# Hybrid decoder step on one Trainium2 core: the order of the first tiles, GpSimd for the sample row, two bursts of decode products, and the last norm

## The chip, the cores and the metric

The kernel runs on one core of one Trainium2 chip. The metric is device time in microseconds of one execution. TensorE (PE) multiplies, VectorE (DVE) and ScalarE (ACT) work on tiles in SBUF and PSUM, GpSimd (POOL) has a queue of stores and some small operations, SyncE (SP) has the queue of most loads. Each engine takes its instructions in a fixed order and waits on semaphores.

## The reference

One layer of a hybrid decoder, for a prompt of 1024 tokens and for 8 samples of one new token each, both with the same weights:

```python
hn = rmsnorm(x, g_norm)                        # x: 1024 x 1024 (prompt), 8 x 1024 (samples)
u = hn @ w_in                                  # 1024 -> 7176 columns
xa, za, uq, uk, uv, uo, zb, ui, uf = split(u)  # seven groups of 1024, two of 4 (gates)
yA = rglru_branch(xa, ...)                     # gated linear recurrence, conv of width 4
h = mlstm_seq(q, k, v, ig, lf, C, n, m)        # 4 heads, chunks of 128 tokens
yB = rmsnorm_per_head(sigmoid(uo) * h) * g_mhead
merged = concat[yA * silu(za), yB * silu(zb)]
x = x + merged @ w_out                         # 2048 -> 1024
y = rmsnorm(x, g_final)
```

Outputs are y and the new states, all in float32.

## The kernel before

**Precision and products.** A float32 product is made of three products of parts (`mm3`, lines 64 to 68: high by high, high by low, low by high). Each operand is split first (`split`, lines 70 to 74): ScalarE casts the high part, VectorE subtracts it to get the low part. The large projections use a Strassen-like scheme of seven block products (`Q_P1` to `Q_P7`) instead of eight, for which sums of the operands' blocks are formed, and split as well.

**Who sets the order.** The program is traced in the order of the Python code, and a planner then gives each engine its fixed order from the tracing order (earlier is more urgent), from data and buffer dependencies and from its own guess of durations. An instruction that is ready in the planner's reckoning may be taken ahead of an earlier one that isn't. `tc.issue_after(ins)` puts what is traced in its block behind `ins` on the engine of `ins`; `tc.manual_schedule` keeps the instructions of its block in tracing order on the engines named, though others may come between them. A pool's tag with n buffers makes the next tile of that tag wait until an older one has been read for the last time.

**The opening (lines 403 to 603).** The prompt is eight tiles of 128 rows, the samples a ninth (number 8, eight rows), taken in the order `xorder = [4, 0, 8, 5, 1, 6, 2, 7, 3]`. For each: `x_fetch` loads it (SP; every third one in a single buffer "xb", the others in the six buffers "ws"); `x_stats` squares and sums on ScalarE and makes the inverse root on both engines; `x_turn` scales by root and norm row on VectorE, then transposes it on PE, in two halves of four blocks, into PSUM; `x_split` splits both halves; `x_copy` keeps plain copies of tiles 4 to 7; `plain` multiplies with the first unit's weights (two value heads, 264 and 256 columns, the first with the 8 gate columns) as 48 products; `x_combos` forms the Strassen sums and splits them. PSUM for the transposes rotates over "kv", "kv", "s", "qp". The norm row is broadcast over the partitions by a product into PSUM (`pb`), and copied to `gn_b` by ScalarE (line 577).

After the ninth tile, the samples' gate product (`pgd`, lines 594 to 599) and `dec_unit(0)` (the samples' products with the first unit's raw weights: 32 matmuls, 64 records in the trace) follow, and then the loads of the next unit's raw weights, whose buffers `dec_unit(0)` reads. In the trace, PE takes the pieces of `dec_unit` where they fit.

**The units (lines 1707 to 1770).** Thirteen more column groups of w_in, seven block products each, with splitting (`prep`), recurrence and decode work between them.

**Attention and output (from line 1774).** The heads and chunks n = 4 to 31 with output products as filling (`fill`). `wo_dec` (lines 1519 to 1529) multiplies the samples' rows with four raw row blocks of w_out at a time, in four column groups of PE at once, and adds the result to a buffer in DRAM. It is called at n = 19 and n = 21. `last_tile` (lines 1646 to 1671) ends the program: last output tile in three column parts (`LP`), sum of squares in three parts, inverse root by logarithm, exponential and one Newton step (`rsqrt_log`), scaling, store.

Of the kernel before, what the change touches and what calls it, by code (L numbers as in the profile page):

```python
# [17 lines left out]
P = 128  # L18
T = 1024
# [32 lines left out]
def hymba_kernel(  # L52
# [17 lines left out]
    def split(hi, lo, src):  # L70

        a = A.copy(hi, src)  # L72
        V.tensor_tensor(lo, src, hi.bitcast(F32), op=ALU.subtract)  # L73
        return a

# [125 lines left out]
    def rsqrt_mean(out, v, t, n):  # L201

        V.tensor_scalar(v, v, 0.25 / n, 0.25 * EPS, op0=ALU.mult, op1=ALU.add)
        rsqrt(out, v, t)

    def rsqrt_log(out, v, t):

        A.activation(t, v, AF.Ln, scale=2.0 ** 32)
        A.activation(out, t, AF.Exp, scale=-0.5)
# [230 lines left out]
    def x_stats(i):  # L440
        n = rows_of(i)
        junk = fp.tile([P, T], BF16, tag="junk", name="junk")
        A.activation(junk[:n], xt[i][:n], AF.Square, accum_out=st0[:n, i, 0:1])
        rsqrt_mean(st0[:n, i, 1:2], st0[:n, i, 0:1], st0[:n, i, 2:3], T)

    def x_turn(m):
        i = xorder[m]
        n = rows_of(i)
        xps[i] = []
        for half in range(2):  # L450
            hs = slice(half * HT, (half + 1) * HT)
            if m == 0 or half == 0:
                s = hs if m == 0 else slice(0, T)
                g = pb[half] if m == 0 else gn_b[:n, s]
                scaled = V.scalar_tensor_tensor(xt[i][:n, s], xt[i][:n, s], st0[:n, i, 1:2], g, op0=ALU.mult, op1=ALU.mult)
            pt = ps(("kv", "kv", "s", "qp")[(2 * m + half) % 4], [P, 4, P])
# [27 lines left out]
    def x_combos(i):  # L484

        p0, p1 = xps[i]
        s = slice(i % 4 * P, (i % 4 + 1) * P)
        f0, f1 = bf["f"]

        def out(q, t):  # L490
            split(cb[q][0][:, :, s], cb[q][1][:, :, s], t)
        if i >= 4:
            t3 = sg([P, 4, P], "t3")
            V.tensor_tensor(t3, f1, f0, op=ALU.subtract)
            out(Q_P7, t3)
        else:
            t1, t2, t4 = (sg([P, 4, P], f"t{n}") for n in (1, 2, 4))
            V.tensor_tensor(t1, f0, p0, op=ALU.subtract)
            V.tensor_tensor(t2, f1, t1, op=ALU.subtract)
            V.tensor_tensor(t4, p1, t2, op=ALU.subtract)  # L500
            out(Q_P6, t2)
            out(Q_P5, t1)
            out(Q_P4, t4)
# [6 lines left out]
    def w1_split(b):  # L510

        t = ws([P, 4, 256], f"w1h{b}"), ws([P, 4, 256], f"w1l{b}")
        split(t[0], t[1], raws[0, b][:, :, 256:512])
        w1.append(t)

# [23 lines left out]

    pw = ps("tr", [P, P])  # L540
# [22 lines left out]
    for m, i in enumerate(xorder):  # L563
        scaled = x_turn(m)
        if m == 0:
            def w0_split(k):
                split(hi[:, k:k + 2, 0:256], lo[:, k:k + 2, 0:256], raws[0, k // 4][:, k % 4:k % 4 + 2, 0:256])
            with tc.issue_after(root.ins), tc.issue_after(scaled.ins):
                w0_split(0)
                split(hi[:, :, 256:264], lo[:, :, 256:264], wg)  # L570
                x_split(i, 0)
                w0_split(2)
            with tc.issue_after(x_split(i, 1).ins):
                w0_split(4)
                w0_split(6)
                for half in range(2):
                    A.copy(gn_b[:, half * HT:(half + 1) * HT], pb[half])
                x_stats(xorder[1])
                for b in range(2):
                    w1_split(b)  # L580
        else:
            x_split(i, 0)
            x_split(i, 1)
        if 4 <= i < 8:
# [5 lines left out]
        if i < 8:  # L590
            plain(i)
            x_combos(i)

    pgd = ps("o", [32, 8])
    for k in range(KC):
        TE.matmul(pgd, hnd[:, NB * k:NB * k + 32], wg[:, k, :], start=k == 0, stop=k == KC - 1)
    gd = dconst([NB, 8], "gd")
    V.tensor_tensor(gd, pgd[0:NB], bgate[0:NB], op=ALU.add)
    ld(d_gd, gd)
    dec_unit(0)  # L600
    load_raw(1, 0)
    load_raw(1, 1)
# [916 lines left out]
    def wo_dec(ms):  # L1519

        po = ps("tr", [P, 512])
        with tc.manual_schedule(engines={mybir.EngineType.PE}):
            for m in ms:
                md = mAd[:, NB * (m % 8):NB * (m % 8) + 32]
                for half in range(2):
                    g = 2 * (m % 2) + half
                    TE.matmul(po[32 * g:32 * g + 32, :], md, oraw[m][:, half * 512:(half + 1) * 512], start=m < ms[2],  # L1527
                              stop=m >= ms[2], skip_group_check=True)
# [117 lines left out]
    def last_tile():  # L1646
# [19 lines left out]
        V.tensor_scalar(ms[:, 0:1], ms[:, 0:1], ms[:, 2:3], 0.25 / T, op0=ALU.add, op1=ALU.mult)  # L1666
        rsqrt_log(ms[:, 4:5], ms[:, 0:1], ms[:, 5:6])
# [112 lines left out]
    for n in range(4, N):  # L1780
# [21 lines left out]
        elif h == 1:  # L1802
            m_zg(c - 1)
            if n == N2 + 3:
                wo_dec((12, 13, 14, 15))
# [12 lines left out]
        else:  # L1818
            fill(1)
            if n == N2 + 1:  # L1820
                wo_dec((8, 9, 10, 11))
# [52 lines left out]
```

## Time and profile before

| | |
|---|---|
| median of three timed runs | 911.5 us (911.31 to 911.98) |
| the profiled execution's own time | 909.62 us |
| its span, first to last instruction | 907.8 us |
| TensorE busy | 895.5 us (99%), clock granted 0.998 |
| VectorE, ScalarE, GpSimd busy | 740.4 (82%), 586.1 (65%), 194.9 us (21%) |

The page's span is shorter than the execution's time by what lies before the first and behind the last instruction. A busy TensorE need not be at its peak: its instructions overlap, so that the distance from one start to the next tells more than a duration. A row of the timeline has start, duration, engine, line, operation, output and inputs, shapes and count, and in brackets the engine's idle time before it and who ended it. A row of a table by stretches has the stretch, its length, then the busy time and the count of instructions of each engine asked for, the granted TensorE clock (1.00 is full), the share of the DMA engines and GB/s.

### The profile page before, as it was taken

To read this page: it belongs to the slowest core of one execution; us is meant where nothing else is said; L and a number is where in the kernel's file an instruction comes from. 1 tells how busy PE (TensorE), PEld (TensorE's weight loads), DVE (VectorE), ACT (ScalarE), POOL (GpSimd) and SP (SyncE) were. 2 spreads that over 40 slices of the span, in tenths; PEclk is the share of its full clock that TensorE was granted. 3 is DMA by queue.
4 is the path that set the end of the run, shared out by engine and by line. 5 is a ranking of instruction groups with operands and counts; after the bars stand their busy time and mean duration, and the time that the engine had idled before them with its cause. 6 is when DMAs were issued, how large, how long until landed. Compare 5 with 4: busy or idle time off the path is not lost. (4 is left out here: it accounts for less than half of the span.)

```text
span 907.8 us, 16671 instructions
## 1 busy us (share of the span) xinstructions
PE 895.5 (99%) x5889; PEld 764.4 (84%) x5889; DVE 740.4 (82%) x1528; ACT 586.1 (65%) x1086; POOL 194.9 (21%) x322
## 2 busy tenths in 40 slices
PE   8999999999999999999999999999999999999996
PEld 6997778887888998888889998887788888888885
DVE  6974779869689978798999877679998779888973
ACT  7663446767667776576768775547787568556652
POOL 1111113012222222323333244010111111111120
PEclk9999999999999999999999999999999999999999
DMA  6412457347556557657585555536689889856531
GB/s 200 152 62 92 140 155 262 112 154 233 192 188 217 179 176 235 202 158 243 188 272 191 193 179 189 170 124 226 202 228 256 203 224 287 216 144 178 178 123 70
DMA packets 127037, 167.76 MB, mean 185 GB/s; under 512 B 17212, under 2 KB 94084, under 8 KB 126946
## 3 DMA queue, kind: packets, MB, share of 16 engines
q1 hardware_dynamic: 105334, 103.68, 37.1%
q0 software_dynamic: 21616, 63.02, 21.6%
q8 instruction: 46, 0.75, 0.4%
q14 instruction: 37, 0.30, 0.1%
q10 hardware_dynamic: 4, 0.00, 0.0%
HBM read 108.00 MB, written 62.92 MB: 188 GB/s over the span
## 5 line engine op out<-in xcount | busy, mean ns | idle before, releaser
L72 ACT CAST wh<-raw 128x1024 fp32r<-128x1024 f32 x91 | 95.4, 1049 | 72.8 <-DVE raw L299 21.2
L73 DVE TENSOR_TENSOR wl<-raw,wh 128x1024 fp32r<-128x1024 f32 x91 | 111.1, 1221 | 36.7 <-ACT wh L72 21.4
L66 PE MATMUL ps_X<-cb_hi,wh 128*128 128x512 f32 x320 | 126.6, 396 | 0.0
L68 PE MATMUL ps_X<-cb_hi,wl 128*128 128x512 f32 x320 | 125.4, 392 | 0.0
L67 PE MATMUL ps_X<-cb_lo,wh 128*128 128x512 f32 x320 | 125.1, 391 | 0.0
L66 PEld LDWEIGHTS ps_X<-cb_hi,wh 128*128 128x128 f32 x320 | 60.1, 188 | 15.9 <-issue 2.5
L68 PEld LDWEIGHTS ps_X<-cb_hi,wl 128*128 128x128 f32 x320 | 60.1, 188 | 13.3 <-issue 0.6
L67 PEld LDWEIGHTS ps_X<-cb_lo,wh 128*128 128x128 f32 x320 | 60.1, 188 | 12.8 <-issue 0.8
L66 PE MATMUL ps_Y<-cb_hi,wh 128*128 128x512 f32 x160 | 63.6, 398 | 0.3 <-DVE s L350 0.3
L68 PE MATMUL ps_Y<-cb_hi,wl 128*128 128x512 f32 x160 | 62.5, 391 | 0.0
L67 PE MATMUL ps_Y<-cb_lo,wh 128*128 128x512 f32 x160 | 62.5, 391 | 0.0
L66 PE MATMUL ps_X<-wh,cb_hi 128*128 128x256 f32 x192 | 54.8, 286 | 0.0
L67 PE MATMUL ps_X<-wl,cb_hi 128*128 128x256 f32 x192 | 54.4, 283 | 0.0
L68 PE MATMUL ps_X<-wh,cb_lo 128*128 128x256 f32 x192 | 54.4, 283 | 0.0
L66 PE MATMUL ps_o<-wo,mh 128*128 128x512 f32 (+1 forms) x136 | 53.1, 391 | 0.0
L68 PE MATMUL ps_o<-wo,ml 128*128 128x512 f32 (+1 forms) x136 | 51.6, 380 | 0.0
L67 PE MATMUL ps_o<-wo,mh 128*128 128x512 f32 (+1 forms) x136 | 51.5, 379 | 0.0
L66 PEld LDWEIGHTS ps_X<-wh,cb_hi 128*128 128x128 f32 x192 | 36.8, 191 | 1.5 <-ACT Z L279 0.4
L67 PEld LDWEIGHTS ps_X<-wl,cb_hi 128*128 128x128 f32 x192 | 36.8, 192 | 0.2
L68 PEld LDWEIGHTS ps_X<-wh,cb_lo 128*128 128x128 f32 x192 | 36.8, 192 | 0.0
L66 PEld LDWEIGHTS ps_Y<-cb_hi,wh 128*128 128x128 f32 x160 | 30.2, 188 | 6.9 <-DVE s L350 0.7
L68 PEld LDWEIGHTS ps_Y<-cb_hi,wl 128*128 128x128 f32 x160 | 30.0, 188 | 6.5
(573 smaller groups left out, 2746.9 us busy)
## 6 DMA issues: line engine op xcount, KB each, us to landing
raw<-in_w_in_dram SPq DMA_DIRECT2D x55, 512.0 KB
Cb<-in_state_mlstm_C_dram SPq DMA_DIRECT2D x32, 256.0 KB
out_dram<-Cb POOLq DMA_DIRECT2D x32, 256.0 KB, 5.0
qk<-d_qk SPq DMA_DIRECT2D x32, 256.0 KB
ring<-d_ro SPq DMA_DIRECT2D x26, 256.0 KB
d_qk<-s POOLq DMA_DIRECT2D x24, 256.0 KB, 4.4
d_x<-s POOLq DMA_DIRECT2D x16, 256.0 KB, 2.5
zsr<-d_y SPq DMA_DIRECT2D x16, 256.0 KB
```

The costliest lines, as they stand in the source:

```text
L66: TE.matmul(out, ah, bh, start=first, stop=False, skip_group_check=True)
L67: TE.matmul(out, ah, bl, start=False, stop=False, skip_group_check=True)
L68: TE.matmul(out, al, bh, start=False, stop=last, skip_group_check=True)
L72: a = A.copy(hi, src)
L73: V.tensor_tensor(lo, src, hi.bitcast(F32), op=ALU.subtract)
```

## The change

- The norm row's two copies go from ScalarE to VectorE, behind the low half of the last weight split. Tile 0's statistics and the splits of the second weight (`w1_split`) get explicit places: the second split stands behind tile 0's root, tile 4's copies and its value copies behind the second split.
- The loop over the tiles is written out for tiles 4, 0 and 5, with statistics of tile 5 behind tile 0's splits, and of tile 1 there too. The samples move behind tile 1: they are multiplied by norm row and root on GpSimd (`x_scale8`), transposed into a buffer of their own ("tr"), and copied by ScalarE. Since they share "xb" with tile 6, that tile's load now depends on them. PSUM for the prompt's tiles alternates between two pairs.
- `x_combos` is parted in `x_sums` and `x_outs`: the sums of tiles 0 and 4 are formed after tile 5's splits, and all splits of sums come one tile later.
- `samples()`, right after tile 1's products, holds `dec_unit(0)` and the gate product in one manually ordered block, the gate store and the loads of unit 1's raw weights.
- `wo_dec` is called once, at n = 21, for all eight row blocks.
- In `last_tile`, the logarithm takes the last part sum directly, with a scale and a bias made from the first two parts; the sum itself is formed beside it, for the Newton step.

```diff
-    def x_turn(m):
+    def x_scale(i, s, g):
+        return V.scalar_tensor_tensor(xt[i][:, s], xt[i][:, s], st0[:, i, 1:2], g, op0=ALU.mult, op1=ALU.mult)
+
+    def x_scale8():
+
+        G.tensor_tensor(xt[8][:NB], xt[8][:NB], gn_b[:NB], op=ALU.mult)
+        G.tensor_scalar(xt[8][:NB], xt[8][:NB], st0[:NB, 8, 1:2], None, op0=ALU.mult)
+
+    def x_turn(m, scale=True):
...
-            pt = ps(("kv", "kv", "s", "qp")[(2 * m + half) % 4], [P, 4, P])
+            if i == 8:
+                if half == 0:
+                    both = ps("tr", [P, 2, 4, 64])
+                pt = both[:, half]
+            else:
+                pt = ps(("kv", "kv", "s", "qp")[(2 * (m - (m > 2)) + half) % 4], [P, 4, P])
...
-            V.tensor_copy(blocks(hnd)[:, 4 * half:4 * half + 4], p[:, :, 0:NB])
+            A.copy(blocks(hnd)[:, 4 * half:4 * half + 4], p[:, :, 0:NB])
...
+    def samples():
+
+        pgd = ps("o", [32, 8])
+        with tc.manual_schedule(engines={mybir.EngineType.PE}):
+            dec_unit(0)
+            for k in range(KC):
+                TE.matmul(pgd, hnd[:, NB * k:NB * k + 32], wg[:, k, :], start=k == 0, stop=k == KC - 1)
+        gd = dconst([NB, 8], "gd")
+        V.tensor_tensor(gd, pgd[0:NB], bgate[0:NB], op=ALU.add)
+        ld(d_gd, gd)
+        load_raw(1, 0)
+        load_raw(1, 1)
...
+    with tc.issue_after(x_split(4, 1).ins):
+        w0_split(4)
+        w0_split(6)
+        with tc.issue_after(low[0].ins):
+            for half in range(2):
+                V.tensor_copy(gn_b[:, half * HT:(half + 1) * HT], pb[half])
+        root = x_stats(0)
+        w1_split(0)
+        with tc.issue_after(root.ins):
+            w1_last = w1_split(1)
+    x_fetch(3)
+    with tc.issue_after(w1_last.ins):
+        x_copy(4)
+        plain(4)
+    x_turn(1)
+    x_split(0, 0)
+    second = x_split(0, 1)
+    x_fetch(4)
+    with tc.issue_after(second.ins), tc.issue_after(low[0].ins):
+        x_stats(5)
+    plain(0)
+    with tc.issue_after(second.ins), tc.issue_after(low[0].ins):
+        x_stats(1)
+    x_turn(3)
+    for m in range(3, 9):
+        i = xorder[m]
+        if m > 3:
+            x_turn(m, m > 4)
+        x_split(i, 0)
+        second = x_split(i, 1)
+        if m == 3:
+            with tc.issue_after(second.ins), tc.issue_after(low[0].ins):
+                x_scale(1, slice(0, T), gn_b)
+                x_stats(8)
+                x_scale8()
+                due = [x_sums(0), x_sums(4)]
+                x_fetch(5)
+        if i >= 4:
             x_copy(i)
         if m + 3 < 9:
             x_fetch(m + 3)
         if m + 2 < 9:
             x_stats(xorder[m + 2])
+        if m == 4:
+            x_turn(2, False)
+            for half in range(2):
+                x_split(8, half)
+        if m > 3:
+            for d in due:
+                x_outs(*d)
+            due = [x_sums(i)]
+        plain(i)
+        if m == 3:
+            due.append(x_sums(i))
+        if m == 4:
+            samples()
+    for d in due:
+        x_outs(*d)
...
-        V.tensor_scalar(ms[:, 0:1], ms[:, 0:1], ms[:, 2:3], 0.25 / T, op0=ALU.add, op1=ALU.mult)
-        rsqrt_log(ms[:, 4:5], ms[:, 0:1], ms[:, 5:6])
+                V.tensor_scalar(ms[:, 0:1], ms[:, 0:1], 0.25 / T, None, op0=ALU.mult)
+                V.tensor_scalar(ms[:, 3:4], ms[:, 0:1], 2.0 ** 32, None, op0=ALU.mult)
+        A.activation(ms[:, 5:6], ms[:, 2:3], AF.Ln, scale=0.25 / T * 2.0 ** 32, bias=ms[:, 3:4])
+        V.tensor_scalar(ms[:, 0:1], ms[:, 2:3], 0.25 / T, ms[:, 0:1], op0=ALU.mult, op1=ALU.add)
+        newton(ms[:, 4:5], ms[:, 0:1], ms[:, 5:6])
...
             if n == N2 + 3:
-                wo_dec((12, 13, 14, 15))
+                wo_dec(range(8, 16))
...
-            if n == N2 + 1:
-                wo_dec((8, 9, 10, 11))
```

`newton` is `rsqrt_log` without its first line, the logarithm.

More of the change, by code (lines that the diff above doesn't have):

```diff
@@ L72, in split @@
         a = A.copy(hi, src)
-        V.tensor_tensor(lo, src, hi.bitcast(F32), op=ALU.subtract)
+        low[:] = [V.tensor_tensor(lo, src, hi.bitcast(F32), op=ALU.subtract)]
         return a
+    low = []
     cpool = ctx.enter_context(tc.tile_pool(name="cpool", bufs=1))
@@ L203, in rsqrt_mean, with newton @@
         V.tensor_scalar(v, v, 0.25 / n, 0.25 * EPS, op0=ALU.mult, op1=ALU.add)
-        rsqrt(out, v, t)
+        return rsqrt(out, v, t)
     def rsqrt_log(out, v, t):
         A.activation(t, v, AF.Ln, scale=2.0 ** 32)
+        newton(out, v, t)
+    def newton(out, v, t):
         A.activation(out, t, AF.Exp, scale=-0.5)
@@ L443, in x_stats @@
         A.activation(junk[:n], xt[i][:n], AF.Square, accum_out=st0[:n, i, 0:1])
[L444 to L446 removed]
+        return rsqrt_mean(st0[:n, i, 1:2], st0[:n, i, 0:1], st0[:n, i, 2:3], T)
+    def x_scale(i, s, g):
[4 more added lines that the diff above has]
+    def x_turn(m, scale=True):
         i = xorder[m]
@@ L449, in x_turn @@
         xps[i] = []
+        scaled = None
         for half in range(2):
             hs = slice(half * HT, (half + 1) * HT)
[L452 to L455, printed above, removed]
-            pt = ps(("kv", "kv", "s", "qp")[(2 * m + half) % 4], [P, 4, P])
+            if m == 0:
+                scaled = x_scale(i, hs, pb[half])
+            elif half == 0 and scale:
+                scaled = x_scale(i, slice(0, T), gn_b)
+            if i == 8:
[4 more added lines that the diff above has]
+                pt = ps(("kv", "kv", "s", "qp")[(2 * (m - (m > 2)) + half) % 4], [P, 4, P])
             for q in range(4):
@@ L482, in x_copy, with x_sums @@
             A.copy(f, p)
-    def x_combos(i):
+    def x_sums(i):
         p0, p1 = xps[i]
-        s = slice(i % 4 * P, (i % 4 + 1) * P)
         f0, f1 = bf["f"]
-        def out(q, t):
-            split(cb[q][0][:, :, s], cb[q][1][:, :, s], t)
         if i >= 4:
@@ L494, in x_combos, with x_outs @@
             V.tensor_tensor(t3, f1, f0, op=ALU.subtract)
[L495 to L503, printed above, removed]
+            return i, [(Q_P7, t3)]
+        t1, t2, t4 = (sg([P, 4, P], f"t{n}") for n in (1, 2, 4))
+        V.tensor_tensor(t1, f0, p0, op=ALU.subtract)
+        V.tensor_tensor(t2, f1, t1, op=ALU.subtract)
+        V.tensor_tensor(t4, p1, t2, op=ALU.subtract)
+        return i, [(Q_P6, t2), (Q_P5, t1), (Q_P4, t4)]
+    def x_outs(i, sums):
+        s = slice(i % 4 * P, (i % 4 + 1) * P)
+        for q, t in sums:
+            split(cb[q][0][:, :, s], cb[q][1][:, :, s], t)
     hi = fp.tile([P, KC, 264], F32R, tag="wph", name="wph")
@@ L512, in w1_split @@
         t = ws([P, 4, 256], f"w1h{b}"), ws([P, 4, 256], f"w1l{b}")
-        split(t[0], t[1], raws[0, b][:, :, 256:512])
         w1.append(t)
+        return split(t[0], t[1], raws[0, b][:, :, 256:512])
     gs = dconst([P, NCH, 8], "gs")
@@ L562, in hymba_kernel, with w0_split @@
     root = x_first_stats()
[L563 to L584, printed above, removed]
+    def w0_split(k):
+        split(hi[:, k:k + 2, 0:256], lo[:, k:k + 2, 0:256], raws[0, k // 4][:, k % 4:k % 4 + 2, 0:256])
@@ new lines, in hymba_kernel @@
+    scaled = x_turn(0)
+    with tc.issue_after(root.ins), tc.issue_after(scaled.ins):
+        w0_split(0)
+        split(hi[:, :, 256:264], lo[:, :, 256:264], wg)
+        x_split(4, 0)
+        w0_split(2)
+    with tc.issue_after(x_split(4, 1).ins):
[8 more added lines that the diff above has]
+            w1_last = w1_split(1)
@@ L589, in hymba_kernel @@
             x_stats(xorder[m + 2])
[L590 to L602, printed above, removed]
+        if m == 4:
[13 more added lines that the diff above has]
+        x_outs(*d)
     es_f.close()
@@ L1526, in wo_dec @@
                     g = 2 * (m % 2) + half
-                    TE.matmul(po[32 * g:32 * g + 32, :], md, oraw[m][:, half * 512:(half + 1) * 512], start=m < ms[2],
-                              stop=m >= ms[2], skip_group_check=True)
+                    TE.matmul(po[32 * g:32 * g + 32, :], md, oraw[m][:, half * 512:(half + 1) * 512], start=m < 10,
+                              stop=m >= 14, skip_group_check=True)
         dec_put(po, accum_op=ALU.add)
```

## The prediction

> **What bounds the kernel now.** I read the page first: its span, its engines.
>
> ```profile
> span 907.8 us, 16671 instructions
> ...
> PE 895.5 (99%) x5889; PEld 764.4 (84%) x5889; DVE 740.4 (82%) x1528; ACT 586.1 (65%) x1086; POOL 194.9 (21%) x322
> ```
>
> TensorE is busy for 99% of the span; what moves the end is PE time. It can be saved in two ways: PE stands idle less, or it does the same work with fewer costly switches. So next come the stretches around the change, PE alone.
>
> ```profile
> 14.16:20.47 6.31, 4.63 (x35) 1.00 0.12 45
> 20.47:72.42 51.95, 51.87 (x472) 1.00 0.33 106
> 72.42:81.40 8.98, 8.90 (x94) 1.00 0.46 137
> ```
>
> The second column is length, then PE's busy time. Idle shows in the first stretch alone, 6.31 - 4.63 = 1.68 us. The timeline tells why.
>
> ```profile
> 10.87 1.08 ACT L577 COPY gn_b<-ps_o 128x512 f32<-128x512 f32 x2
> ...
> 11.82 1.08 ACT L443 ACTIVATE junk<-x 128x1024 bf16<-128x1024 f32 x1
> ...
> 12.87 1.05 ACT L72 CAST w1h<-raw 128x1024 fp32r<-128x1024 f32 x1
> ...
> 13.02 0.15 DVE L203 TENSOR_SCALAR st<-st 128x1 f32<-128x1 f32 x1 [1.15 <-ACT junk L443]
> ...
> 13.96 1.23 DVE L73 TENSOR_TENSOR w1l<-raw,w1h 128x1024 fp32r<-128x1024 f32 x1 [0.78 <-ACT w1h L72]
> 14.04 0.28 PE L68 MATMUL ps_o<-wph,cb_lo 128*128 128x264 f32 x1
> ...
> 14.16 0.28 PE L66 MATMUL ps_o<-w1h,b12h 128*128 128x256 f32 x1
> ...
> 15.24 0.39 PE L67 MATMUL ps_o<-w1l,b12h 128*128 128x256 f32 x1 [0.79 <-DVE w1l L73]
> ...
> 17.51 1.26 DVE L455 SCALAR_TENSOR_TENSOR x<-x,st,gn_b 128x1024 f32<-128x1024 f32 x1
> ...
> 18.79 1.06 ACT L443 ACTIVATE junk<-x 128x1024 bf16<-128x1024 f32 x1
> 18.83 0.66 PE L459 MATMUL ps_s<-idF,x 128*128 128x128 f32 x4 [0.35 <-DVE x L455]
> ...
> 20.47 0.39 PE L66 MATMUL ps_o<-wph,cb_hi 128*128 128x264 f32 x1 [0.54 <-ACT cb_hi L72]
> ```
>
> PE starts a product every 0.12 us (14.04 to 14.16), then stands three times: for the low half of the second weight (15.24), for the scaled tile 0 (18.83), for its cast (20.47). Each traces back to ScalarE doing the norm row's copies at 10.87 first, and squaring tile 5 at 18.79 before tile 0's cast.
>
> **The change, part by part.**
>
> *Norm row on VectorE, sums apart (14 to 25 us).* The copies (1.08 us) leave ScalarE; VectorE has 1.15 us idle at the same place (the 13.02 row), and two copies of 512 from PSUM should fit there as they did on ScalarE: cost nothing, the cover being that hole. Tile 0's square moves from 11.82 to 10.87, w1h from 12.87 to 11.8 at best. But its data must be there:
>
> ```profile
> DMA  1999996101675116971911461111010021013970
> ```
>
> In this row (first 80 us in 40 slices) the DMA engines are full until 12 us. So w1h gains between nothing and 1.07; I take 0.8, a cast from about 12.05. Then w1l ends near 14.4 instead of 15.2, the second w1l near 16.1, and the scaling of tile 0, no longer behind tile 4's difference of 0.6 us, ends near 17.45 instead of 18.77. Transposes start near 17.6 instead of 18.83; the square of tile 5 now stands behind tile 0's second cast, so the cast starts 0.65 after the first transpose and not 1.0. First product of tile 0: near 18.9 instead of 20.47, -1.6 us. Bounds: -0.3 (weights late) and -1.68 (all the idle).
>
> *Tile 5 and the first unit's decode products (25 to 72 us).*
>
> ```profile
> 26.89 1.28 DVE L455 SCALAR_TENSOR_TENSOR x<-x,st,gn_b 128x1024 f32<-128x1024 f32 x1
> 27.22 1.06 PE L274 MATMUL ps_tr<-raw,hnd 128*32 128x128 f32 x26
> ...
> 28.32 0.63 PE L459 MATMUL ps_s<-idF,x 128*128 128x128 f32 x4
> ```
>
> Tile 5 is scaled only at 28.17, since VectorE splits tile 0's sums first; PE fills the hole with decode pieces. With the sums put off, tile 5 is scaled by about 23. The pieces, by stretch, line 274 alone, the last row a later unit's whole burst:
>
> ```profile
> 27.22:31.31 4.09, 1.89 (x36) 1.08 (x36) 1.00 0.25 64
> 59.20:60.34 1.14, 0.77 (x12) 0.29 (x12) 1.00 0.00 0
> 71.83:72.42 0.59, 0.59 (x16) 0.39 (x16) 1.00 0.00 0
> 73.09:79.44 6.35, 2.49 (x64) 1.75 (x64) 1.00 0.65 194
> 605.02:606.90 1.88, 1.88 (x64) 1.69 (x64) 1.00 0.37 141
> ```
>
> Unit 0's 64 records take 1.89 + 0.77 + 0.59 = 3.25 us in pieces, a burst 1.88: -1.37. The product behind a burst comes late:
>
> ```profile
> 606.90 0.50 PE L66 MATMUL ps_X<-cb_hi,wh 128*128 128x512 f32 x1
> 607.24 0.40 PE L67 MATMUL ps_X<-cb_lo,wh 128*128 128x512 f32 x1
> 607.48 0.40 PE L68 MATMUL ps_X<-cb_hi,wl 128*128 128x512 f32 x1
> ```
>
> 0.34 instead of 0.24: a switch costs 0.1 on each side. Some three piece ends next to products vanish, -0.4; together -1.8. What the pieces covered is then open: between a tile's last transposes and its first product PE waits for a transpose's end and a cast (about 0.4), and after four products for the low half (0.15). Tile 1's transposes can't fill in, because they need the PSUM pair that now holds tile 0 until its sums are taken. Tile 5 pays 0.55 and tile 3 0.4: +0.95. Tile 1's gap is filled by the sample's transposes, which only move.
>
> PE's new clock from there: tile 0's products take 6.1 (the stretch from 20.47 to 27.22 without 0.6 of the sample's transposes) and end at 25.0; tile 5 takes 0.9 for transposes, 0.55 idle and 48 times 0.12, to 32.25; tile 1's transposes end at 33.2, the sample's at 33.7, tile 1's products at 39.6, burst and gate products (2.5) at 42.1.
>
> *The sample on GpSimd, and what is queued behind it.* Its VectorE scaling (1.27) goes; two GpSimd operations and two ScalarE copies come.
>
> ```profile
> 19.78 1.27 DVE L455 SCALAR_TENSOR_TENSOR x<-x,st,gn_b 8x1024 f32<-8x1024 f32 x1
> ...
> L134 POOL TENSOR_SCALAR_AFFINE_SELECT maskT<-maskT 128x128 f32<-128x128 f32 x1 | 0.3, 284 | 0.0
> ```
>
> No row has GpSimd arithmetic of this width. Bounds for one of 1024: VectorE's 1.27, and 284 ns times 8, 2.3 us. I take 1.8 each, nearer the GpSimd row: squared at about 28.1 (behind tile 5's casts), the sample is ready near 32.4. PE reaches it behind tile 1's transposes, about 33.2: no wait. The stores of tile 5's values stand behind the two on GpSimd's queue, and nobody reads these before the attention; the two ScalarE copies have only value copies behind them.
>
> But tile 6 shares the sample's buffer, so its load, on SP's queue, now waits for the sample's transposes at 33.7:
>
> ```profile
> 21.83 0.33 SPq L418 DMA_DIRECT2D x<-in_x_prompt_dram  x1
> ...
> 29.41 0.33 SPq L418 DMA_DIRECT2D x<-in_x_prompt_dram  x1
> ...
> 33.15 1.06 ACT L443 ACTIVATE junk<-x 128x1024 bf16<-128x1024 f32 x1 [0.21 <-DMA x<-in_x_prompt_dram]
> ```
>
> Before, it was fetched at 21.83. A load takes 3.7 us (29.41 to 33.15); beside tile 7's I take 4.2. Issued near 34.0, tile 6 lands near 38.2; square and accumulator 1.25, the root's chain about 1.1 and the scaling 1.28 make it ready at 41.9 at best, with VectorE shared 42.5. PE is done with tile 1's products and the burst at about 42.1: +0.4, bounds 0 and 2.
>
> By the first unit's first product (72.42 before): -1.6 - 1.8 + 0.95 + 0.4 = -2.05; I take -1.9, since tile 0's low half, once covered by the sample's transposes, leaves PE 0.15 idle.
>
> *Unit 1.* Its second raw half was loaded only after unit 0's last decode pieces; now both loads (and the sample's gate store) move up SP's queue from 72 to 42, past tile 3's load, which PE needs 15 us later, so its burst need not wait for data: 2.49 in three pieces becomes 1.88, and four switches go: -0.9. Bounds 0 (the planner still uses it as filling, which then covers the idle charged above) and -1.1.
>
> *Output weights' decode products.* Two bursts
>
> ```profile
> 782.36 1.92 PE L1527 MATMUL ps_tr<-oraw,mAd 128*32 128x512 f32 x16
> ...
> 796.25 1.92 PE L1527 MATMUL ps_tr<-oraw,mAd 128*32 128x512 f32 x16
> ```
>
> become one of 32: the work stays, one pair of switches goes, -0.3 (0 to -0.35). One ScalarE copy and one GpSimd store go too, off PE's path. PE work that covered the waits at 782 is gone there; other fills are left, at nothing.
>
> *The end.*
>
> ```profile
> 901.28 0.19 ACT L1662 ACTIVATION_READ_ACCUMULATOR ps_o<-y 128x1 f32 x1
> 901.50 0.21 DVE L1666 TENSOR_SCALAR ms<-ms 128x1 f32<-128x1 f32 x1
> 901.75 0.20 ACT L208 ACTIVATE ms<-ms 128x1 f32<-128x1 f32 x1 [0.28 <-DVE ms L1666]
> 901.98 0.20 ACT L209 ACTIVATE ms<-ms 128x1 f32<-128x1 f32 x1
> ```
>
> The logarithm takes the third part sum itself, so line 1666 leaves the path: one ScalarE step follows another in 0.23 (901.75 to 901.98), so 901.75 becomes 901.50: -0.25 (0 to -0.25). The two added VectorE operations lie before the last products' end or beside the logarithm.
>
> **Sum:** -1.9 - 0.9 - 0.3 - 0.25 = -3.35, say -3.2 for what a planner rearranges. The profiled execution took 909.62 us (span 907.8), so 906.4 there; the three timed runs have a median of 911.5, 1.9 higher, so the prediction is 911.5 - 3.2 = 908.3. About 0.2% (1.8 us) is what can be told from no change.
>
> **The rivals.**
>
> *GpSimd holds VectorE up.* Tile 1's transposes need tile 0's three sums, done near 31.0 against a need at 32.25. If VectorE can't run beside a GpSimd operation, one or two of them (1.8 each) push the sums to 32.8 or 34.6, and the sample, tile 6's load and its scaling follow: PE stands 0.6 to 2.3 at tile 1. Against it: 1.2 us of slack. For it: VectorE, 82% busy on the average, has most of its work in these stretches. Time: 911.5 - 3.2 + 1.7 = 910.0. The Trainium skill, "SBUF — State Buffer", section "Who interferes with whom", says that a VectorE instruction with two SBUF inputs and a GpSimd one that reads SBUF block one another; the scaling of tile 1 and the second sum are of that kind. By that rule the sum would be this rival's -1.5, by the row of 284 ns alone the forecast's -3.2; no run here shows it so far.
>
> *The gain isn't there.* The weights land later than 12 us, and the burst is broken by the planner as before (the order fixed inside it doesn't keep others out): -0.3 for the start, +0.5 for pieces and new idle, -0.3 for unit 1 and -0.5 for output and end make -0.6: 910.9. For it: the full DMA engines.
>
> *Slower: the sample late in PE's order.* PE's order is fixed beforehand. If the sample's transposes are placed behind tile 1's products, at 39.6 instead of 33.2, tile 6 is fetched at 40.2, lands at 44.2 and is scaled near 48, while PE has work until 42.7 only: 5.2 us idle, which is 2.0 more than the gain: 913.5. It decides from 3.2 + 1.8 = 5.0 us on. Against it: tile 1's cast leaves PE a hole just there. For it: two operations of unknown length on GpSimd, whose cost the planner only guesses.
>
> **How the numbers follow.** Forecast 0.62, GpSimd 0.17, no gain 0.10, sample late 0.11. The range reaches from 906.6 (new idle filled, tile 6 on time) to 911.6 and leaves out the slower case and little else; the forecast's own range is 906.6 to 909.7. Faster by over 0.2% (under 909.7): 0.62 and a third of the GpSimd case, 0.68; within: 0.21; slower: 0.11.
>
> **What would show it.** The wait before the first product with w1l at most 0.3; tile 0's first product near 18.9; tile 5's transposes straight behind tile 0's products, no decode record ahead of them; one run of 64 records of line 274 near 40; the first unit's first product near 70.5 and its second group (81.40 before) near 78.6; 32 records of the output decode in one run; 0.25 less between the last accumulator and the logarithm. Wrong it would be by an idle PE ahead of tile 6's transposes, by a sample that PE waits for, or by new stalls after 80 us, where I expect the same order of work.

## The result, and the profile after

The changed kernel takes 917.88 us (median; 916.44 to 919.30) beside 911.74 us of the kernel before (911.31 to 912.32) on the same chip: ratio 1.0068, 95% interval 1.0055 to 1.0081, so 6.1 us slower where 3.2 us faster was forecast. The profiled execution, the fastest of six, took 916.44 us; its span is 914.7 us.

First the stretches of PE that answer to the three shown of before (up to tile 0's first product, the first unit, and unit 1 to its second product group), and two stretches inside the first unit. Columns: length, PE busy, granted clock, DMA share, GB/s.

```profile
14.16:18.81 4.65, 4.41 (x38) 1.00 0.16 63
18.81:82.02 63.21, 57.13 (x537) 0.95 0.33 106
82.02:87.87 5.85, 5.85 (x27) 1.00 0.06 22
...
32.32:38.04 5.72, 1.04 (x10) 0.96 0.31 93
38.04:50.73 12.69, 12.04 (x137) 0.75 0.25 69
```

The opening is 1.66 us shorter (6.31 before), unit 1 3.13 us shorter (8.98 before; its decode products now lie in the first unit), and the first unit 11.26 us longer (51.95 before): together 6.47 us. The two lower rows say where: PE worked 1.04 us of 5.72, and the next 12.69 us were granted a clock of 0.75. What PE waited for, between 17 and 83 us (total, times, longest):

```profile
PE ps_tr L479 <- POOL x L458: 4.7, 1, 4.7
PE ps_kv L479 <- DVE x L453: 0.7, 1, 0.7
...
```

The transposes of the sample (L479 into ps_tr) wait 4.7 us for GpSimd. The timeline of the chain that leads there, and of tile 6 behind it:

```profile
27.75 3.17 POOL L457 TENSOR_TENSOR x<-x,gn_b 8x1024 f32<-8x1024 f32 x1 [1.42 <-ACT junk L449]
...
29.34 2.13 DVE L514 TENSOR_TENSOR t<-b22f,t 128x512 f32<-128x512 f32 x1
...
32.13 0.14 DVE L233 RECIPROCAL st<-st 8x1 f32<-8x1 f32 x1
...
32.45 5.53 POOL L458 TENSOR_SCALAR x<-x,st 8x1024 f32<-8x1024 f32 x1 [1.01 <-DVE st L233]
...
45.59 0.37 ACT L554 COPY pe<-ps_o 128x256 f32<-128x256 f32 x1 [3.67 <-PE ps_o L68]
...
46.38 1.06 ACT L449 ACTIVATE junk<-x 128x1024 bf16<-128x1024 f32 x1
```

GpSimd's two operations take 3.17 and 5.53 us, not 1.8 each. The second can start only when the sample's root is there (32.13), so the sample is ready at 37.98, while PE stood before it from 33.4. The root is late itself: its last steps stand on VectorE behind the product at 29.34, which took 2.13 us beside GpSimd's first operation. Tile 6, whose load waits for the sample's transposes, is then late as well: its square (46.38) stands on ScalarE behind the copy of tile 1's first values (45.59), which the slow products delayed, and PE waits another 0.7 us for it.

The end of the program:

```profile
908.30 0.30 ACT L1728 ACTIVATE ms<-ms 128x1 f32<-128x1 f32 x1
```

This is the logarithm. From the last accumulator's start (908.08) to the last scaling (909.50) it takes 1.42 us. Before, the accumulator stood at 901.28 and the scaling at 902.85: 1.57. In between, up to the attention stage, every stretch of the units is as far behind as at 82 us (6.0 to 6.5 us). In the attention stage this execution loses another 0.8 us, and the single burst of output decode products returns 0.33.

### The profile page after: what moved, and what is told of

Same layout as the page of the kernel before. It is cut to its first block, busy times and chain, and to the rows that moved or that the text cites. A ratio compares the mean times of both kernels' runs of the same rounds, so it can differ in the third digit from the quotient of the medians.

```text
span 914.7 us, 16678 instructions
## 1 busy us (share of the span) xinstructions
PE 897.7 (98%) x5889; PEld 767.9 (84%) x5889; DVE 742.5 (81%) x1529; ACT 585.2 (64%) x1085; POOL 203.3 (22%) x323
```

## The experiments

The theory (A): GpSimd's result is late, PE stands idle, and the idle time lowers the clock behind it. The rivals: the new order of the work costs by itself (B); GpSimd holds VectorE up (C); the clock has nothing to do with the wait (D). Each ratio is to the kernel before, run on the same chip.

### One VectorE operation for the sample

```diff
-        G.tensor_tensor(xt[8][:NB], xt[8][:NB], gn_b[:NB], op=ALU.mult)
-        G.tensor_scalar(xt[8][:NB], xt[8][:NB], st0[:NB, 8, 1:2], None, op0=ALU.mult)
+        V.scalar_tensor_tensor(xt[8][:NB], xt[8][:NB], st0[:NB, 8, 1:2], gn_b[:NB], op0=ALU.mult, op1=ALU.mult)
```

> The changed kernel with the sample scaled by one VectorE operation (root and norm row at once, as before the change) in the place of the two GpSimd ones; all else as changed. Theory A (the loss of 6.1 us is the late sample: 4.7 us of PE waiting, then about 3.2 us because 12.7 us were granted a clock of 0.75, then 0.8 us for tile 6): VectorE can scale at 32.1 when the root is there, 1.27 us, ready 33.5 against PE at 33.3, so the wait falls to about 0.3, the clock stays at 1.00, tile 6 waits 0.3 at most: 917.9 - 4.4 - 3.2 - 0.6 = 909.7, 908.5 to 910.5. Theory B (the new order itself costs: sums late, no decode pieces to fill with, other order in the later stages): at most the 4.7 us come back and new waits open: 912 to 914.

Measured: 909.96 us beside 910.56, ratio 0.9993 (0.9984 to 1.0001). Against the changed kernel's 1.0068 that is 6.8 us back from two lines. The ranges were reckoned from 917.9 us, beside a kernel before of 911.74: as ratios A's is 0.9964 to 0.9986 and B's 1.0003 to 1.0025. So the time lies between them, and A expected more to come back than did. The rows decide for A's mechanism: the wait for the sample is gone, and with it more than the whole loss, so B is out as its cause. The waits of PE between 26 and 90 us, two rows of VectorE in the opening, and a row of VectorE and one of PE much later:

```profile
PE ps_kv L478 <- DVE x L453: 0.9, 1, 0.9
PE ps_o L66 <- ACT b12h L72: 0.5, 2, 0.2
```

```profile
29.49 0.69 DVE L513 TENSOR_TENSOR t<-b22f,t 128x512 f32<-128x512 f32 x1
...
30.83 0.14 DVE L233 RECIPROCAL st<-st 8x1 f32<-8x1 f32 x1
...
132.54 0.55 DVE L877 TENSOR_SCALAR xc<-xs,PT 128x512 f32<-128x512 f32 x1 [1.12 <-DMA xs<-d_x]
...
133.74 0.50 PE L66 MATMUL ps_Y<-cb_hi,wh 128*128 128x512 f32 x1 [1.42 <-DVE s L356]
```

Nothing waits for GpSimd any more. Without GpSimd beside it the product that took 2.13 us takes 0.69, and the root is there at 30.83 instead of 32.13, although tile 5 was scaled 0.15 us later here (27.54 against 27.39): GpSimd's first operation had put it off by some 1.4 us. But the gain that is left is 0.6 us, not 3.2. Unit 1's second product group comes at 80.33, 1.07 before its old place, and at 133.74 PE gives nearly all of that back: it waits 1.4 us for a VectorE sum that stands behind a block loaded from DRAM at 132.5. The block's load was issued 1.3 us earlier than before the change (126.37 against 127.70), but its reader started only 0.1 us earlier (132.64 before).

### One GpSimd operation

```diff
-        G.tensor_scalar(xt[8][:NB], xt[8][:NB], st0[:NB, 8, 1:2], None, op0=ALU.mult)
+        A.mul(xt[8][:NB], xt[8][:NB], st0[:NB, 8, 1:2])
```

> The changed kernel with GpSimd's first operation (norm row, 3.17 us) kept and the second (root, 5.53 us) replaced by one ScalarE multiplication. Theory A: the norm row is done at 30.9, before the root at 32.3, so the first operation is not on the path; ScalarE's multiplication takes about 1.1 us and stands among casts, ready near 33.8: wait about 0.5 instead of 4.7, no drop of the clock: 909.8, 908.8 to 911. The VectorE operation of 2.13 us beside GpSimd's first operation should still be there. Theory C (GpSimd beside VectorE is what costs, by the first operation as well): the root stays late, PE still waits over 1.5 us: 911.5 to 914.

Measured: 910.58 beside 910.56, ratio 1.0002 (0.9993 to 1.0010). Nearly all of the loss is back. As a ratio the time lies above A's range (0.9968 to 0.9992) and in C's (0.9997 to 1.0025), but PE waits 0.3 us for the sample, as A says, and not over 1.5: it was the second operation that made the sample so late. A's "no drop of the clock" was wrong, at least in the profiled execution, which took 911.78, above the median. Stretches of 3.4 us, first of the changed kernel, then of this one:

```profile
34.08:37.49 3.41, 0.00 (x0) 1.00 0.51 154
37.49:40.90 3.41, 2.86 (x22) 0.51 0.35 77
40.90:44.32 3.42, 3.42 (x16) 0.50 0.32 122
```

```profile
32.68:36.09 3.41, 2.51 (x22) 1.00 0.51 147
36.09:39.50 3.41, 3.41 (x18) 0.51 0.57 207
```

The clock falls to half in steps of 3.4 us: two steps behind 4.7 us of waiting, one step here, though PE was busy for 2.51 of the 3.41 us ahead of it (1.2 of that with transposes). 18 products in 3.41 us instead of 28 cost about 1.2 us. The Trainium skill, "TensorE: Matmul & The Clock Gate", section "Part 1: The HAM clock gate (the "warmup" mystery)", says that the gate halves the clock by activity in free-running windows of about 3.4 us, after an idle one. The length agrees with these rows; that a window has to be idle does not, since PE was busy for most of the one ahead of the drop here. Nor does the idle time alone decide. In the run with the sums split later (below) PE was busy for less, and the clock stayed:

```profile
31.80:35.20 3.40, 1.81 (x16) 1.00 0.25 81
35.20:38.60 3.40, 2.71 (x23) 1.00 0.57 190
```

What the gate counts is not shown by these runs.

### PE kept busy while it waits

```diff
...
+            with tc.issue_after(turned[0].ins):
+                idle = ps("tr", [P, P])
+                for _ in range(19):
+                    last = TE.matmul(idle, ones, ones, start=True, stop=True)
-            x_turn(2, False)
+            with tc.issue_after(last.ins):
+                x_turn(2, False)
```

> The changed kernel with 19 products of ones (128x128, written to a spare PSUM tile that nobody reads) between tile 1's transposes and the sample's, so that PE is busy while it waits for GpSimd; one product of tile 1 falls between them and the sample's transposes. Theory A (the clock drops because PE stood idle): the sample is as late as before, but the stretch behind it is granted 1.00 instead of 0.75, 3.2 us less: 914.7, 914 to 915.5. Theory D (the clock has nothing to do with the idle time, or the half-rate products cost nothing since others were late anyway): 917 to 918.5.

Measured: 914.14 beside 910.56, ratio 1.0040 (1.0028 to 1.0051): 2.5 us less than the changed kernel's loss. GpSimd takes 5.53 us again, and the sample is transposed 0.45 us later than before (38.49 against 38.04), but PE is busy (19 products, two records each):

```profile
33.64 4.41 PE L653 MATMUL ps_tr<-ones 128*128 128x128 f32 x38
...
38.49 0.66 PE L481 MATMUL ps_tr<-idF,x 8*128 8x8 f32 x8 [0.32 <-POOL x L458]
```

```profile
32.32:38.04 5.72, 5.72 (x53) 1.00 0.35 117
38.04:50.73 12.69, 12.01 (x159) 1.00 0.47 148
```

The clock of the second stretch is 1.00 where it was 0.75. So useless products made the kernel faster than the changed one, and the loss of 6.1 us parts into some 2.5 us of clock and 3.6 us that the late sample costs in other ways. D is out.

### The late parts alone

In the kernel before, the output weights' decode products at n = 21 for all eight row blocks, and the new end; nothing else.

> The kernel before with the two late parts of the change alone: the output weights' decode products in one burst, and the shorter end. Theory A: 0.33 and 0.15 us less: 911.2, 910.9 to 911.5. Theory E (the 0.7 us that the changed kernel lost in the attention stage, between 673 and 735 us, come from the moved burst): 911.9 or more, with the same loss at the same place.

Measured: 910.13 beside 910.56, ratio 0.9997 (0.9989 to 1.0006): in the direction of A's -0.48 and too small to tell from nothing. The trace is clearer: 32 records in one run, and an end of 1.41 instead of 1.57 us (901.48 to 902.89).

```profile
L1531 PE MATMUL ps_tr<-oraw,mAd x32: 592/592/617, 794.7 to 797.7; 128*32 128x512 f32 x32
```

In this execution PE lost 0.5 us at 756 us, ahead of the moved burst, where it waited for a VectorE difference (Cl, line 73), and got 0.32 back by the burst. Whether the wait comes from the move isn't shown. Between 673 and 735 us it lost nothing, so E, as far as it names that place, is out.

### A buffer of its own for the sample

On top of the first experiment, tile 6 goes into one of the six shared buffers:

```diff
-... if m % 3 == 2 else ws([P, T], f"x{i}", F32)
+... if m in (2, 8) else ws([P, T], f"x{i}", F32)
```

> The changed kernel with the sample scaled by one VectorE operation (as in e1_vector), and tile 6 loaded into one of the six shared buffers, so that its load no longer waits for the sample's transposes. In e1_vector PE still waited 0.86 us for tile 6 (scaled at 43.7 against PE's 42.9). Theory A (that wait is the price of the shared buffer): it goes, the first unit's second product group starts 0.9 us earlier than in e1_vector (79.4 against 80.33), and the time falls to 909.1 (908.6 to 909.6) beside e1_vector's 909.96 and the kernel before's 910.56. Theory G (a gain of the opening is given back at the third column unit, where in e1_vector PE waited 1.4 us for a VectorE sum that stands behind a loaded block xs at 132.5): the second group is earlier, but the time stays at 909.7 to 910.3.

Measured: 909.55 beside 910.90, ratio 0.9992 (0.9983 to 1.0001). The wait for tile 6 is gone, yet the product group came at 80.83 instead of the expected 79.4. A new wait, larger than the old one, stands at the same tile:

```profile
46.08 0.38 PE L280 MATMUL ps_tr<-raw,hnd 128*32 128x128 f32 x2 [1.16 <-DMA raw<-in_w_in_dram]
```

The planner filled tile 6's hole with two records of unit 1's decode products, whose weights were still on their way. The time is in G's range, but neither A nor G holds as written: the gain went to a new wait in the opening itself, and at 133 us nothing more was lost.

### GpSimd kept, PE given other work first

The two GpSimd operations stay, tile 6 has its shared buffer, and the sample's transposes are put behind the 39th of tile 1's 48 products.

> The changed kernel with both GpSimd operations kept as they are, tile 6 loaded into a shared buffer, and the sample's eight transposes put behind the 39th of tile 1's 48 products instead of ahead of them. Theory A (GpSimd's 8.7 us cost only because PE's next instruction needed them): the sample, ready at 38, is reached by PE at about 39.3, no wait, no low clock: 909.3, 908.6 to 910.2, within 0.5 of e5_own_buffer. Theory C (GpSimd at work beside VectorE holds VectorE up: one operation took 2.13 instead of 0.67 us in the changed kernel): sums and splits come late, PE waits over 1 us at tile 1 or 6, and the time is 910.6 to 912.

Measured: 910.29 beside 910.90, ratio 0.9998 (0.9989 to 1.0007), 0.7 us above the fifth experiment: between the two theories. Nothing waits for the sample, and the clock stays up; but the next waits are those of C. PE's waits between 26 and 80 us, and rows of both engines:

```profile
PE ps_o L66 <- ACT cb_hi L72: 1.9, 2, 1.5
PE ps_o L68 <- DVE cb_lo L73: 0.8, 1, 0.8
```

```profile
32.93 3.06 POOL L458 TENSOR_SCALAR x<-x,st 8x1024 f32<-8x1024 f32 x1
...
33.32 1.47 DVE L73 TENSOR_TENSOR cb_lo<-t,cb_hi 128x512 fp32r<-128x512 f32 x1
...
35.38 0.67 DVE L73 TENSOR_TENSOR cb_lo<-t,cb_hi 128x512 fp32r<-128x512 f32 x1
```

A VectorE difference that takes 0.67 us (35.38) takes 1.47 beside the start of GpSimd's second operation (33.32). PE waits 1.5 us for tile 1's cast and 0.8 for its low half. Not all of the 1.5 is lateness: tile 1's first product stands 2.58 us behind its first transpose, against 2.00 in the fifth experiment, where the sample's transposes filled a part of that gap. And the form that took 5.53 us takes 3.06 here, though VectorE worked on such differences and sums beside it, too. That raised the next question: what is GpSimd's own price?

### GpSimd's price, alone and beside VectorE

Operations on junk behind the last store of the kernel before, first with 512 elements:

> The kernel before with ten more operations behind its last store, on junk: on 8 and then on 128 partitions of 512 elements, GpSimd's product of two tiles, its product with a number per partition and its product with a constant, and on VectorE, started at the same time, the product of two tiles and the one with a number per partition. The time of the run means nothing, the rows do. Theory A (5.53 and 3.17 us for 1024 elements are the prices of these forms by themselves): half of that for 512, 2.8 us with a number per partition and 1.6 us for two tiles, on 8 and on 128 partitions alike. Theory C (they were long because VectorE was at work): at most 1.6 us for the form with a number per partition where VectorE is idle. Beside GpSimd's product of two tiles VectorE's own should take over 1 us instead of 0.69, by the 2.13 us seen in the changed kernel.

```profile
903.73 0.68 DVE L1676 TENSOR_TENSOR y<-yg,gf 8x512 f32<-8x512 f32 x1 [0.27 <-ACT yg L1669]
...
905.63 1.63 POOL L1674 TENSOR_SCALAR y<-yg,ms 8x512 f32<-8x512 f32 x1
905.84 1.07 DVE L1676 TENSOR_TENSOR y<-yg,gf 128x512 f32<-128x512 f32 x1
...
910.32 1.56 POOL L1674 TENSOR_SCALAR y<-yg,ms 128x512 f32<-128x512 f32 x1
```

1.6 us on 8 partitions and on 128, not 2.8: A's half of 5.53 is wrong. VectorE's product of two tiles, which began 0.05 us ahead of GpSimd's, took 0.68 and not over 1 us; the one that began 0.21 us behind a GpSimd operation (905.84) took 1.07. So being side by side isn't enough to be held; the two rows speak for the order of beginning. Then with 1024 elements, each begun together with a row of VectorE operations:

> The kernel before with eight GpSimd operations of 8x1024 on junk behind its last store, each begun together with VectorE: the product of two tiles four times, then the product with a number per partition four times; each time first with VectorE idle, then with four VectorE products of two SBUF tiles (128x512) started at once, then the same four behind one VectorE product with an input from PSUM, then six with an input from PSUM. The time of the run means nothing, the rows do. In the changed kernel the form with a number per partition took 5.53 us, with VectorE at products of two SBUF tiles all the while, in e6_hidden 3.06. Theory H (VectorE's products of two SBUF tiles hold GpSimd off, or are held off, whoever comes first; PSUM inputs don't matter): alone about 3.1 us, behind four such products that start first about 3.1 + 2.6 = 5.7, and with PSUM inputs 3.1 again; where GpSimd starts first, VectorE's first product of two SBUF tiles takes 2 us or more instead of 0.69. Theory A (5.53 us is this form's own price on 1024 elements): 5.5 us in all four cases.

```profile
907.48 2.33 POOL L1685 TENSOR_TENSOR oraw<-oraw 8x1024 f32<-8x1024 f32 x1 [12.64 <-DVE oraw L1691]
908.09 4.45 DVE L1679 TENSOR_TENSOR y<-yg,gf 128x512 f32<-128x512 f32 x4
...
917.05 2.85 POOL L1687 TENSOR_SCALAR oraw<-oraw,ms 8x1024 f32<-8x1024 f32 x1 [2.03 <-DVE oraw L1691]
...
920.01 3.65 DVE L1679 TENSOR_TENSOR y<-yg,gf 128x512 f32<-128x512 f32 x4
920.19 3.21 POOL L1687 TENSOR_SCALAR oraw<-oraw,ms 8x1024 f32<-8x1024 f32 x1 [0.28 <-DVE oraw L1691]
...
923.83 2.83 POOL L1687 TENSOR_SCALAR oraw<-oraw,ms 8x1024 f32<-8x1024 f32 x1 [0.43 <-DVE oraw L1691]
924.42 3.23 DVE L1679 TENSOR_TENSOR y<-yg,gf 128x512 f32<-128x512 f32 x4
...
927.81 2.83 POOL L1687 TENSOR_SCALAR oraw<-oraw,ms 8x1024 f32<-8x1024 f32 x1 [1.15 <-DVE oraw L1691]
```

The product of two tiles takes 2.33 us where VectorE was reading PSUM when it began (first row), and the form with a number per partition 2.85 beside an idle VectorE. Four VectorE products of two SBUF tiles, 2.86 us undisturbed, become 4.45, 3.65 or 3.23. With PSUM inputs (last row) GpSimd takes 2.83, as when alone. So H is right in kind, and it missed the size: four products that began ahead of GpSimd held it for 0.36 us, not 2.6, and four that began 0.6 us behind it didn't hold it at all. The planner put the product of two tiles with an idle VectorE, and with one that starts first, into the attention stage (2.40 us at 800.5 and 2.79 at 804.6), away from the VectorE products meant to stand beside it, so these two show nothing of the kind.

### Sums split later

The changed kernel, with the splits of three tiles' sums behind the copies of the transposed sample:

```diff
...
-            for d in due:
-                x_outs(*d)
+            with tc.issue_after(copied.ins):
+                for d in due:
+                    x_outs(*d)
```

> The changed kernel with both GpSimd operations, and the splits of the sums of tiles 0, 4 and 5 put behind ScalarE's copies of the transposed sample, so that VectorE has two products of two SBUF tiles (instead of seven) while GpSimd multiplies by the root. Behind idle or PSUM-reading VectorE the form took 2.83 us in e8_who_waits, beside four products of two SBUF tiles 3.21, in e6_hidden 3.06, in the changed kernel 5.53. Theory J (a longer row of VectorE's products of two SBUF tiles holds GpSimd off): 2.8 to 3.4 us here, the sample ready at 35.7 instead of 38.0, PE waits 2.4 us instead of 4.7, and the time is 912 to 914.5 beside 910.7 of the kernel before. Theory K (VectorE has no part in it): 5.3 to 5.7 us again, and 915.5 to 917.5.

```profile
32.71 3.12 POOL L458 TENSOR_SCALAR x<-x,st 8x1024 f32<-8x1024 f32 x1 [1.02 <-DVE st L233]
```

```profile
PE ps_tr L479 <- POOL x L458: 2.3, 1, 2.3
```

3.12 us instead of 5.53 and a wait of 2.3 instead of 4.7: the rows are J's, and K is out. The 2.4 us between them go when the splits go, which are VectorE's differences and, with them, some casts on ScalarE; the test above, where VectorE alone was beside GpSimd, speaks for VectorE, though with a smaller size. The time, 915.38 beside 910.63 (ratio 1.0058, 1.0037 to 1.0080), is above J's range and just under K's. The profiled execution took 911.8 us with a clock of 0.998 over the span; the other three took 913.9, 916.8 and 917.7 with 0.994, 0.993 and 0.993. So the same kernel ends 1.2 us behind the kernel before in one execution and 7.0 in another, and the slower ones were granted less clock; where they lost it has no trace.

### Unit 1's decode products later

On top of the fifth experiment, they are put behind the last product of the seventh tile, or all behind that of the last tile:

```diff
...
-            dec_unit(u)
+            with tc.issue_after(lastp[2].ins):   # or lastp[3]
+                dec_unit(u)
```

> e5_own_buffer, with unit 1's decode products put behind the last product of the seventh tile (number 2), so that none of them stands in PE's order before their weights are there (in e5_own_buffer PE waited 1.2 us for them at tile 6). Theory A (that wait is what kept e5_own_buffer from its gain): PE gains 1.2 us there, loses up to 0.4 at one tile where the pieces covered a cast: the second product group of the first column unit at 79.9 (80.83 there, 81.40 before), time 0.9 below e5_own_buffer's: 0.22% below the kernel before, 908.3 to 909.5. Theory G (gains of the opening are given back later): group at 79.9, time within 0.4 of e5_own_buffer's.

> e5_own_buffer, with all of unit 1's decode products behind the last product of the last tile: 64 records in one run of 1.88 us, as the prediction had it for unit 1. Theory A (pieces between products cost 0.3 to 0.4 us a time for switches, and the holes that they fill, each about 0.4 us, are as large): like e9_mended within 0.5 us; group at 79.8 to 80.2. Theory I (the burst is better, as the prediction's term of -0.9 had it): 0.5 us or more below e9_mended.

Measured: 910.04 beside 910.67, ratio 0.9992 (0.9983 to 1.0001), and 909.89, ratio 0.9989 (0.9980 to 0.9998). The wait for weights is gone in both, and the product group still comes at 80.8 and 81.1, not at 79.9. So A of the first is out, and between A and I of the second the time is for A: 0.15 us lie between the two versions. In the first a wait of 0.79 us for a cast (52.19) took the place of the wait for weights. The second is the version in which the change's steps stand nearest to what the prediction meant, apart from the sample, which is on VectorE and off tile 6's buffer, and from unit 0's decode products, which stand in two runs of 20 and 44 records. It shows their sum (stretches as above, then PE's waits between 17 and 83 us):

```profile
14.16:18.69 4.53, 4.29 (x37) 1.00 0.12 44
18.69:74.91 56.22, 53.79 (x537) 1.00 0.36 119
74.91:81.10 6.19, 6.09 (x30) 1.00 0.06 21
```

```profile
PE ps_o L66 <- ACT cb_hi L72: 1.7, 4, 0.8
PE ps_o L66 <- ACT b12h L72: 0.5, 2, 0.2
PE ps_kv L482 <- DVE x L457: 0.4, 1, 0.4
```

The first unit is 56.22 us long with unit 1's burst of 1.89 in it: 54.33 without, where it was 51.95. PE stands 2.43 us in it, where it stood 0.08 before (51.95 - 51.87). The decode products of unit 0 alone did get cheaper, 0.78 + 1.50 = 2.28 us in their two runs where they took 3.25; PE's other work took as much more, and why isn't shown. This is the one version whose interval lies below 1, and only just (0.9998). The medians of the first and the fifth experiment and of the two here lie within 0.04% of each other, so that none of them is shown to be better than the rest.

### The norm row alone

In the kernel before, its two copies on VectorE, nothing else.

> The kernel before with one edit: the norm row's two copies on VectorE instead of ScalarE. Theory A (ScalarE's copies stand in front of tile 0's square and of the second weight's cast): the wait of 0.79 for that weight's low half falls to 0.3, tile 0's first product comes 0.3 to 0.8 us earlier than 20.47 (its cast still stands behind tile 5's square), and if it holds to the end the time falls by as much: 909.9 to 910.4 beside 910.7. Theory G (a gain in the opening comes back as another wait before 82 us): first product earlier, second product group of the first column unit within 0.3 of 81.40, time within 0.3 of the kernel before.

```profile
20.32 0.39 PE L66 MATMUL ps_o<-wph,cb_hi 128*128 128x264 f32 x1 [1.11 <-ACT cb_hi L72]
```

Measured: 910.78 beside 910.63, ratio 1.0000 (0.9990 to 1.0009): G. The wait for the second weight is gone, and tile 0's first product is 0.15 us earlier; the rest went to its cast, which still stood behind tile 5's square and made PE wait 1.11 us. The 1.66 us of the changed kernel's opening need the edits to the order too.

## Why the prediction was wrong, point by point

- **The start: right.** Forecast first product of tile 0 at 18.9, measured 18.81; tile 5's transposes straight behind tile 0's products, no decode record ahead of them.
- **The step that failed: "I take 1.8 each, nearer the GpSimd row ... the sample is ready near 32.4 ... no wait".** It priced the two operations as if GpSimd worked by itself, from another engine and from another operation on another shape, and put their meeting with VectorE into a rival. They took 3.17 and 5.53 us, and the sample was ready at 37.98. Without VectorE's two-tile work beside them they take 2.33 and 2.85, at and above the upper bound of 2.3. The 4.7 us that PE waited can be parted from the rows, as an estimate. Some 2.7 us are the second operation's 5.53 instead of 2.85. Some 1.4 us are the root, which came late because GpSimd's first operation held the VectorE product ahead of its last steps. About 0.5 us are left, by which the sample would have been late at the operations' own prices (a root at 30.7, the second operation from 31.0 to 33.85, PE from 33.4). So even the price alone was too low, but most of the wait is contention in both directions.
- **The clock: not in the prediction.** It priced a late sample at its wait. Behind the wait the clock was at half for 6.8 us; that is some 2.5 us of the 6.1.
- **The load behind the sample: mechanism right, size off.** Forecast +0.4 within 0 to 2. In the first experiment, with the sample in time, tile 6 cost 0.9; with a buffer of its own nothing, and PE then waited elsewhere.
- **The first unit's decode products: "together -1.8" and "+0.95" of new idle time.** Both were wrong. In the one-burst version the unit comes out 2.4 us longer, where the terms of the unit made it 0.3 shorter. PE's idle time there is 2.43 us, more than twice the forecast: the pieces had filled holes that ScalarE's casts leave at each tile, and I counted two such holes, where the waits name six. And the busy time did not fall by 1.8, or at all (53.79 less the burst of 1.89 is 51.90, before 51.87), although the decode products themselves took 2.28 instead of 3.25. The sign "one run of 64 records near 40" failed as well: in the changed kernel the planner put 10 of them at 40.16, 51 at 48.08 and 3 at 49.52, as the rival "the gain isn't there" had it.
- **Unit 1: -0.9, right where done as told.** In the one-burst version 6.19 + 1.89 - 8.98 = -0.90. In the changed kernel the planner used the products as filling again, the bound that I had put at nothing: their 64 records (line 280) take 2.87 us between 50.73 and 82.02, in the first unit, and 5.85 + 2.87 - 8.98 = -0.26.
- **Output weights -0.3: right (0.33). The end -0.25: 0.15**, because the logarithm with a bias takes 0.30 instead of 0.20.
- **The rivals.** "The sample late in PE's order" named the place and the sign, with a wrong path: PE's order was as forecast, and PE waited in it. For 5.2 us of idle time it gave 2.0 us more than before; PE waited 5.4 us (4.7 and 0.7), and the time rose by 6.1, since the clock and the first unit's missing gain weren't in it. "GpSimd holds VectorE up" was there (2.13 us instead of 0.69 at 29.34), on another path: tile 1's transposes did not wait for the sums (32.32), but the sample's root came 1.4 us later. The reverse, GpSimd held up beside VectorE, cost 2.4 us by the run with the splits later, 2.7 by the price alone, and was in no rival. The Trainium skill, "SBUF — State Buffer", section "Who interferes with whom", says that a VectorE operation with two SBUF inputs and a GpSimd operation that reads SBUF contend, and that the order of issue decides who is held. In kind the rows agree. In size they don't decide: the operation of 5.53 us began beside a VectorE product, as the one of 3.21 us in the test and the one of 3.06 with PE given other work first did, and what made one wait through several products and the others through part of one isn't shown.

What stays open: that last point; what the clock gate counts; and most of the 0.8 us which the profiled execution of the changed kernel lost between 673 and 735 us. A wait of 0.23 us for ScalarE (733.37) is the only one with a name there.

## What to carry to other kernels

Where an operation moves to an engine on which the trace has no row of its form, take the forecast's worst case from a decision, not from an average: ask when the consumer needs it, and whether the change holds at twice or three times your price. Ask also what the engine that it meets will lose, and what stands behind that. Where PE is 99% busy, an idle gap has two prices, its length and the clock behind it, and the second can differ from one execution to the next: the kernel with a gap of 2.3 us took 911.8 us once and 913.9 to 917.7 three times. And work that fills holes is worth what the holes are worth: before small pieces are gathered into a burst, count the holes that they filled, by the waits that will stand there.

## What was not expected of the hardware

- The granted clock went to half for whole steps of 3.4 us: in one kernel behind a step in which PE was busy 2.51 of 3.41 us, in the changed kernel behind one in which it was not busy at all, and for a second step there behind one, at half clock itself, with 2.86 us of work. Behind a step with only 1.81 us of work, in a third kernel, it stayed at 1.00. Products of the same form started every 0.22 us instead of 0.12.
- GpSimd's product with a number per partition takes 1.6 us for 512 elements per partition, on 8 partitions as on 128 (1.63 and 1.56), and 2.85 for 1024 on 8. Moving eight rows to it saves nothing by their being few.
- With a row of VectorE operations on two SBUF tiles beside it a GpSimd operation took 5.53 us, with fewer of them 3.1, by itself 2.85; one GpSimd operation stretched a VectorE product from 0.69 to 2.13. VectorE products with an input from PSUM did neither (2.83 us for GpSimd's operation beside six of them).
